# Inverting the triangular matrices of a gated delta rule by 32- and 64-blocks on parts of the PE array

## The chip, the cores and the metric

The kernel runs on one core of one Trainium2 chip. The metric is the device time of one execution in microseconds. Five engines work beside each other, each in the order of its own queue: TensorE (PE; PEld is its loading of weights), VectorE (DVE), ScalarE (ACT), GpSimd (POOL) and SyncE (SP), which here starts the DMAs.

## The reference

The network has two parts of two layers each, for 256 tokens of width 1024 in float32. The changed code serves the mixers of the first part, in which a gated delta rule runs beside a retention. For each of 8 heads and each chunk of tokens the reference solves a unit lower triangular system:

```python
a_mat = jnp.einsum("bhnid,bhnjd->bhnij", kb, kc) * jnp.where(strict, decay_incl, 0.0)
lhs = jnp.eye(CHUNK, dtype=jnp.float32) + a_mat
u = lax.linalg.triangular_solve(lhs, vc * bc, left_side=True, lower=True, unit_diagonal=True)
w = lax.linalg.triangular_solve(lhs, kb * jnp.exp(gc)[..., None], left_side=True, lower=True, unit_diagonal=True)
...
v_new = un - jnp.einsum("bhcd,bhdv->bhcv", wn, S)
o = jnp.einsum("bhcd,bhdv->bhcv", qd, S) + jnp.einsum("bhij,bhjv->bhiv", qkn, v_new)
```

The kernel computes the same with chunks of 128 tokens, so that there are two chunks, and with an explicit inverse of each chunk's 128x128 matrix. Outside the mixers the network has a dense feed-forward layer, a mixture of experts, a gated linear recurrence (hgrn), an attention and two more feed-forward layers; the change does not touch them.

## The kernel before

Weights come from memory in tiles of 1 MB (raw). ScalarE rounds each to whi, VectorE forms the rest wlo (parts, L242 to L265), and every product with a weight is three matmuls of such parts with 256 moving columns, which a program calls ws (L280) and tok (L304). The order of TensorE's instructions is the order of the program, written out by hand; the other engines' queues are ordered by a planner with its own model of costs. Small pieces of work are Python generators in a list; after each half of a projection tick (L135) moves every generator on by one step, so that their matmuls stand between those of the projections.

In a mixer (L457) four pairs p of heads go through three such generators. chains (L486) builds, for each head and chunk, the strictly triangular 128x128 matrix, in U (planes 0 and 2 are the diagonal chunks, plane 1 couples the two chunks). inverses (L494) inverts the 32x32 blocks on the diagonals of two pairs at once on VectorE (invert32, L764) and leaves the blocks in iXc and transposed in iXT. solve (L507) then takes pair by pair. invert_begin (L787) lets GpSimd spread the blocks to block-diagonal 128x128 matrices X and XT and lets VectorE mask U in two ways (Um: what couples 32-blocks, and what couples 64-blocks). invert (L802) then goes up two levels. On each, the product of Um with X and an identity added by a bf16 matmul gives V, which ScalarE evicts; on the first level XT and V give the new X (px), and on both V and XT give the new XT (pxt). Each of these has four matrices of 128x128: two heads and two chunks. gdn_out (L723) uses XT: z is the solution of the first chunk, which changes the right side of the second chunk, and so on. After the first z it begins the next pair (then, L734). The tile z had the same buffer as X.

The steps (yield) of invert separate its groups: one before the first, two between V and px, one each after.

Of the kernel before, what the change touches and what calls it, by code (L numbers as in the profile page):

```python
# [7 lines left out]
F32 = mybir.dt.float32  # L8
# [4 lines left out]
OP = mybir.AluOpType  # L13
# [10 lines left out]

C_ID, C_M, C_TRI, C_NEG, C_IOTA = range(5)
NCONST = 5
C1_LV = 0
C1_GM = 2 * 128
C1_RET = 3 * 128
C1_COS = C1_RET + 4 * 256  # L30
C1_SIN = C1_COS + 256
# [53 lines left out]
class Net:  # L85
# [637 lines left out]
    def gdn_out(self, l, st, begun, then, sgz, p, ga):  # L723
        mp = self.mp
        U, Q, vt, fq = st
        XT = yield from self.invert(*begun)

        z = mp.tile([128, 2, 2, 128], F32, tag="X", name="z", bufs=1)
        pz1 = self.pss("pz1")
        for h in range(2):  # L730
            self.mmul(pz1[:, h * 128:(h + 1) * 128], XT[:, h, 0, :], vt[:, 0, h, :])
        self.act(z[:, 0, :, :], pz1[:, :256].rearrange("p (a b) -> p a b", b=128))
        yield
        then()  # L734
        pz2 = self.pss("pz2")
        for h in range(2):
            self.mmul(pz2[:, h * 128:(h + 1) * 128], U[:, h, 1, :], z[:, 0, h, :])
        v2 = vt[:, 1, :, :]
        self.tt(v2, v2, pz2[:, :256].rearrange("p (a b) -> p a b", b=128), OP.subtract)
        yield  # L740
        pz3 = self.pss("pz3")
        for h in range(2):
            self.mmul(pz3[:, h * 128:(h + 1) * 128], XT[:, h, 1, :], vt[:, 1, h, :])
        self.act(z[:, 1, :, :], pz3[:, :256].rearrange("p (a b) -> p a b", b=128))
        yield

        po = self.pss("pog")
        for h in range(2):
            self.mmul(po[:, h * 128:(h + 1) * 128], Q[:, h, 0, :], z[:, 0, h, :])
            self.mmul(po[:, (2 + h) * 128:(3 + h) * 128], Q[:, h, 1, :], z[:, 0, h, :], start=True, stop=False)  # L750
            self.mmul(po[:, (2 + h) * 128:(3 + h) * 128], Q[:, h, 2, :], z[:, 1, h, :], start=False, stop=True)
        o = mp.tile([128, 1536], F32R, tag="uq", name="go", bufs=4, odd=True)
        o = o[:, :512], o[:, 512:1024]
        while p not in sgz:
            yield

        def tail():
            yield from self.head_out(po, fq, sgz[p].rearrange("p t (h d) -> p t h d", h=2), mp, o, 0,
                                     [self.gdn_g[:, l:l + 1]])
            ga[p] = self.as_act(*o)  # L760

        self.bg.append(tail())

    def invert32(self, n, inv):  # L764


        nc, mp = self.nc, self.mp
        A = self.qk("iA").rearrange("p a b (c i) -> p (a b c) i", i=32)
        X = mp.tile([128, 32, 8], F32, tag="iX", name="iX", bufs=1)
        y = mp.tile([128, 160], F32, tag="iY", name="iY", bufs=1)  # L770
        nc.sync.dma_start(X, self.i["cst4"].rearrange("p (i c) -> p i c", c=8))
        nc.vector.transpose(A.rearrange("p i (b r) -> p i b r", r=4),
                            self.Uc.rearrange("p b i -> p i b")[:, :, :, None].to_broadcast([128, 32, 8, 4]))
        for j in range(31):
            a, m = 31 - j, j // 4 + 1
            yj = y[:, :a * m].rearrange("p (i c) -> p i c", c=m)
            self.tt(yj, A[:, j + 1:, j:j + 1].to_broadcast([128, a, m]), X[:, j:j + 1, :m].to_broadcast([128, a, m]),
                    OP.mult)
            self.tt(X[:, j + 1:, :m], X[:, j + 1:, :m], yj, OP.subtract)
            if j % 5 in (1, 3):  # L780
                yield
        Xc, XTc = (mp.tile([128, 8, 32], F32, tag=t, name=t, bufs=1) for t in ("iXc", "iXT"))
        nc.vector.transpose(Xc.rearrange("p b (c r) -> p c b r", r=4), X.rearrange("p i c -> p c i"))
        nc.vector.transpose(XTc, Xc)
        inv[n] = Xc, XTc

    def invert_begin(self, U, Xc, XTc, p):  # L787

        mp = self.mp
        Ud = U[:, :, 0:3:2, :]  # L790
        gm = self.c1[:, C1_GM:C1_GM + 128].rearrange("p (g i) -> p g i", g=4)[:, None, :, :].to_broadcast([128, 4, 4, 32])
        X, XT = (mp.tile([128, 2, 2, 128], F32, tag=n, name=n, bufs=b) for n, b in (("X", 1), ("XT", 2)))
        Um = [mp.tile([128, 2, 2, 128], F32, tag="Um", name="Um", bufs=2) for _ in range(2)]
        for dst, src in ((X, Xc), (XT, XTc)):
            self.nc.gpsimd.tensor_tensor(dst.rearrange("p a b (g i) -> p (a b) g i", g=4),
                                         src[:, 4 * p:4 * p + 4, None, :].to_broadcast([128, 4, 4, 32]), gm, op=OP.mult)
        for s in range(2):
            lv = self.c1[:, C1_LV + 128 * s:C1_LV + 128 * (s + 1)]
            self.tt(Um[s], Ud, lv[:, None, None, :].to_broadcast([128, 2, 2, 128]), OP.mult)
        return X, XT, Um  # L800

    def invert(self, X, XT, Um):  # L802

        mp = self.mp
        flat = lambda x: x.rearrange("p a b c -> p (a b c)")
        yield
        for s in range(2):
            pv = self.pss("pinv")
            for b in range(4):
                o = pv[:, b * 128:(b + 1) * 128]  # L810
                self.mmul(o, Um[s][:, b // 2, b % 2, :], X[:, b // 2, b % 2, :], start=True, stop=False)
                self.mmul(o, self.idb, self.idb, start=False, stop=True)
            V = mp.tile([128, 2, 2, 128], F32, tag="Um", name="V", bufs=2)
            self.act(flat(V), pv)
            yield
            if not s:
                yield
            if not s:
                px = self.pss("px")
                for b in range(4):  # L820
                    self.mmul(px[:, b * 128:(b + 1) * 128], XT[:, b // 2, b % 2, :], V[:, b // 2, b % 2, :])
                X = mp.tile([128, 2, 2, 128], F32, tag="X", name="X", bufs=1)
                self.act(flat(X), px)
            pt = self.pss("pxt")
            for b in range(4):
                self.mmul(pt[:, b * 128:(b + 1) * 128], V[:, b // 2, b % 2, :], XT[:, b // 2, b % 2, :])
            XT = mp.tile([128, 2, 2, 128], F32, tag="XT", name="XT", bufs=2)
            self.act(flat(XT), pt)
            yield
        return XT  # L830

    def ret_pair(self, l, p, u, w, rq, rk, rv, rg, rets):
# [823 lines left out]
def consts():  # L1656
    import numpy as np
    j = np.arange(128)[:, None]
    i = np.arange(128)[None, :]
    c = np.zeros((128, NCONST, 128), np.float32)  # L1660
# [4 lines left out]
    c[:, C_IOTA] = i  # L1665
    c1 = np.zeros((128, N_C1), np.float32)
    c1[:, C1_GM:C1_GM + 128] = j // 32 == i // 32
    for n in range(2):
        s = 32 << n
        m = (j // (2 * s) == i // (2 * s)) & ((i // s) % 2 == 1) & ((j // s) % 2 == 0)  # L1670
        c1[:, C1_LV + 128 * n:C1_LV + 128 * (n + 1)] = -m.astype(np.float32)
    lg = np.log1p(-np.exp2(-5.0 - np.arange(4)))
    for h in range(4):
        for b in range(2):
# [174 lines left out]
```

## Time and profile before

| | |
|---|---|
| median of 3 runs | 2286.77 us (2286.52 to 2286.87) |
| profiled execution | 2284.09 us |
| its span | 2282.2 us |
| TensorE busy | 2205.0 us, 97% |
| VectorE busy | 1694.3 us, 74% |
| ScalarE busy | 1282.9 us, 56% |
| GpSimd busy | 170.0 us, 7% |

The span runs from the first to the last instruction of the profiled execution. A busy time counts the time in which an engine works on at least one instruction. Matmuls overlap: one with 256 moving columns is listed with 0.28 us, but the next begins 0.12 us later, so the cost of a group of matmuls is read from starts, not from durations. A float32 matmul appears as two records of TensorE. In a form such as `128*32 128x64` the first pair is rows by columns of the array, the second the output. The name of a tile stands without its buffer number.

### The profile page before, as it was taken

What the parts mean: (1) busy time and instruction counts of PE and PEld (TensorE: products, weight loads), DVE (VectorE), ACT (ScalarE), POOL (GpSimd) and SP (SyncE); (2) the same over time, 40 slices, a digit from 0 to 9 for tenths busy, and PEclk for the clock granted to TensorE, in tenths of its full rate; (3) what the DMA queues carried; (4) which work ended last, traced back from release to release, by engine and by line L of the source; (5) the groups of instructions that cost most, each with busy time, mean ns of one, the idle gap of its engine ahead of it and who ended that gap; (6) DMA issues with size and microseconds to landing.
All of it is one profiled execution on the core that took longest, in us unless ns stands there. A gap on an engine that the chain in (4) does not pass through costs nothing.

```text
span 2282.2 us, 38609 instructions
## 1 busy us (share of the span) xinstructions
PE 2205.0 (97%) x15571; PEld 2044.7 (90%) x15571; DVE 1694.3 (74%) x2596; ACT 1282.9 (56%) x1992; POOL 170.0 (7%) x142
## 2 busy tenths in 40 slices
PE   8999999999999999989999999989999999999998
PEld 7998998997899899978888887888898799998997
DVE  6878667776587885679999998686777666666554
ACT  5655545443556554468787776554644555556443
POOL 0032100000003210000000000331000000000000
PEclk9999999999999999999999999999999999999999
DMA  7443566887454356769999996344687564444553
GB/s 235 148 140 122 185 221 209 264 272 257 134 184 147 114 172 200 252 225 370 316 359 335 328 340 235 118 135 149 199 272 277 193 198 147 149 148 139 185 181 133
DMA packets 338525, 478.57 MB, mean 210 GB/s; under 512 B 9874, under 2 KB 239116, under 8 KB 338340
## 3 DMA queue, kind: packets, MB, share of 16 engines
q1 hardware_dynamic: 338340, 476.05, 62.2%
q8 instruction: 123, 2.02, 0.4%
q14 instruction: 62, 0.51, 0.1%
HBM read 474.95 MB, written 1.06 MB: 209 GB/s over the span
## 4 chain that ended last, share of the span: by engine, by line
issue 31%; PE 21%; DVE 2%; POOL 1%; ACT 1%; POOLq 0%; DVEq 0%; ACTq 0%
PE peg L171 5%; PE peu L171 5%; PE pey L171 5%; DVE wlo L159 1%; PE phg L171 1%; PE pgat L171 1%; PE pf L171 1%; PE po L171 1%; PE phv L171 1%; PE phq L171 1%; PE pho L171 1%; POOL ms L346 0%; PE psc L171 0%; POOL rs L177 0%; PE pht L174 0%
## 5 line engine op out<-in xcount | busy, mean ns | idle before, releaser
L159 DVE TENSOR_TENSOR wlo<-raw,whi 128x1024 fp32r<-128x1024 f32 (+2 forms) x802 | 929.7, 1178 | 306.4 <-ACT whi L156 296.8
L156 ACT ACTIVATE whi<-raw 128x1024 fp32r<-128x1024 f32 (+3 forms) x828 | 832.6, 1023 | 517.0 <-PE po L171 61.5
L171 PE MATMUL pu<-uh,whi 128*128 128x256 f32 x480 | 134.6, 280 | 0.0
L171 PE MATMUL pg<-uh,whi 128*128 128x256 f32 x480 | 134.2, 280 | 0.0
L171 PE MATMUL pu<-ul,whi 128*128 128x256 f32 x480 | 134.2, 280 | 0.0
L171 PE MATMUL pg<-ul,whi 128*128 128x256 f32 x480 | 134.1, 279 | 0.0
L171 PE MATMUL pu<-uh,wlo 128*128 128x256 f32 x480 | 133.9, 279 | 0.0
L171 PE MATMUL pg<-uh,wlo 128*128 128x256 f32 x480 | 133.8, 279 | 0.0
L346 POOL TENSOR_SCALAR ms<-ss 128x1 f32<-128x1 f32 x30 | 16.5, 549 | 1485.5 <-ACT junk L156 1479.7
L168 DVE SCALAR_TENSOR_TENSOR acc<-raw,cond,acc 128x1024 f32<-128x1024 f32 x84 | 108.4, 1291 | 17.3 <-DMA raw<-in_ada_w_dram 16.5
L171 PE MATMUL paq<-uh,whi 128*128 128x256 f32 x384 | 111.0, 289 | 0.0
L171 PE MATMUL pqkv<-uh,whi 128*128 128x256 f32 x384 | 108.8, 283 | 0.0
L171 PE MATMUL pqkv<-uh,wlo 128*128 128x256 f32 x384 | 107.1, 279 | 0.0
L171 PE MATMUL paq<-ul,whi 128*128 128x256 f32 x384 | 107.1, 279 | 0.0
L171 PE MATMUL pqkv<-ul,whi 128*128 128x256 f32 x384 | 107.0, 279 | 0.0
L171 PE MATMUL paq<-uh,wlo 128*128 128x256 f32 x384 | 107.0, 279 | 0.0
L171 PE MATMUL po<-whi,fh 128*128 128x512 f32 x264 | 103.1, 391 | 2.0 <-DVE fm L168 2.0
L171 PE MATMUL po<-wlo,fh 128*128 128x512 f32 x264 | 103.0, 390 | 0.7 <-DVE wlo L159 0.7
L171 PE MATMUL po<-whi,fl 128*128 128x512 f32 x264 | 102.8, 389 | 0.0
L171 PEld LDWEIGHTS pg<-uh,whi 128*128 128x128 f32 x480 | 90.2, 188 | 0.9 <-ACT fh L156 0.9
L171 PEld LDWEIGHTS pu<-uh,whi 128*128 128x128 f32 x480 | 90.2, 188 | 0.9 <-ACT whi L156 0.9
L171 PEld LDWEIGHTS pg<-uh,wlo 128*128 128x128 f32 x480 | 90.0, 187 | 0.0
(470 smaller groups left out, 6548.9 us busy)
## 6 DMA issues: line engine op xcount, KB each, us to landing
raw<-in_w_in_dram SPq DMA_DIRECT2D x70, 1024.0 KB
raw<-in_ada_w_dram SPq DMA_DIRECT2D x48, 1024.0 KB
raw<-in_ffn_w_in_dram SPq DMA_DIRECT2D x44, 1024.0 KB
raw<-in_attn_w_in_dram SPq DMA_DIRECT2D x36, 1024.0 KB
raw<-in_exp_w_gate_dram SPq DMA_DIRECT2D x32, 1024.0 KB
raw<-in_exp_w_up_dram SPq DMA_DIRECT2D x32, 1024.0 KB
raw<-in_exp_w_down_dram SPq DMA_DIRECT2D x32, 1024.0 KB
raw<-in_ffn_w_out_dram SPq DMA_DIRECT2D x20, 1024.0 KB
```

Of the source, the lines that this page charges most:

```text
L156: self.nc.scalar.activation(out, in_, func, scale=scale, bias=bias, **k)
L159: self.nc.vector.tensor_tensor(out, a, b, op=op)
L168: self.nc.vector.scalar_tensor_tensor(out, a, s, b, op0=op0, op1=op1)
L171: self.nc.tensor.matmul(out, lhsT, rhs, start=start, stop=stop, skip_group_check=skip)
L346: self.nc.gpsimd.tensor_scalar(ms, self.ss[:, t, 0:1], self.ss[:, t, 1:2], EPS, op0=OP.add, op1=OP.add)
```

## The change

All four matrices' 32-blocks and 64-blocks are now multiplied as such, on the part of the array that the partitions of their operands select. invert_begin makes no Um; GpSimd spreads X only to 64x64 blocks on the first 64 partitions, and XT as before. invert has the same steps with the same four groups: eight 32x32 products of U with iXc directly, negated on the way out of PSUM, one half by ScalarE, the other by VectorE (V); twelve 32x32 products for the new off-diagonal blocks, of X for the upper half alone and of XT for both halves; four 64x64 products for V2; four for the last block of XT. Only new blocks are evicted, into X and XT in place. iXc and iXT have two buffers, z one of its own. The two masks leave the table of constants, whose size stays.

```diff
-        z = mp.tile([128, 2, 2, 128], F32, tag="X", name="z", bufs=1)
+        z = mp.tile([128, 2, 2, 128], F32, tag="z", name="z", bufs=1)
...
-        Xc, XTc = (mp.tile([128, 8, 32], F32, tag=t, name=t, bufs=1) for t in ("iXc", "iXT"))
+        Xc, XTc = (mp.tile([128, 8, 32], F32, tag=t, name=t, bufs=2) for t in ("iXc", "iXT"))
...
     def invert_begin(self, U, Xc, XTc, p):
-        for dst, src in ((X, Xc), (XT, XTc)):
-            self.nc.gpsimd.tensor_tensor(dst.rearrange("p a b (g i) -> p (a b) g i", g=4),
-                                         src[:, 4 * p:4 * p + 4, None, :].to_broadcast([128, 4, 4, 32]), gm, op=OP.mult)
-        for s in range(2):
-            lv = self.c1[:, C1_LV + 128 * s:C1_LV + 128 * (s + 1)]
-            self.tt(Um[s], Ud, lv[:, None, None, :].to_broadcast([128, 2, 2, 128]), OP.mult)
-        return X, XT, Um
+        X = mp.tile([64, 4, 64], F32, tag="X", name="X", bufs=1)
+        XT = mp.tile([128, 2, 2, 128], F32, tag="XT", name="XT", bufs=2)
+        Xc, XTc = (x[:, 4 * p:4 * p + 4, :] for x in (Xc, XTc))
+        for dst, src, n, g in ((X, Xc, 64, 2), (XT.rearrange("p a b c -> p (a b) c"), XTc, 128, 4)):
+            self.nc.gpsimd.tensor_tensor(dst.rearrange("p b (g i) -> p b g i", g=g),
+                                         src[0:n, :, None, :].to_broadcast([n, 4, g, 32]),
+                                         gm[0:n, None, 0:g, :].to_broadcast([n, 4, g, 32]), op=OP.mult)
+        return U, Xc, XTc, X, XT
...
-    def invert(self, X, XT, Um):
+    def invert(self, U, Xc, XTc, X, XT):
         mp = self.mp
-        flat = lambda x: x.rearrange("p a b c -> p (a b c)")
+        T3 = XT.rearrange("p a b c -> p (a b) c")
+        part = lambda b, r, c: U[r, b // 2, 2 * (b % 2), c]
         yield
-        for s in range(2):
-            pv = self.pss("pinv")
+        pv = self.pss("pinv").rearrange("p (b c) -> p b c", b=4)
+        V = mp.tile([128, 4, 32], F32, tag="V", name="V", bufs=1)
+        pairs = [(slice(64 * g, 64 * g + 32), slice(64 * g + 32, 64 * g + 64)) for g in range(2)]
+        for r1, r2 in pairs:
             for b in range(4):
-                o = pv[:, b * 128:(b + 1) * 128]
-                self.mmul(o, Um[s][:, b // 2, b % 2, :], X[:, b // 2, b % 2, :], start=True, stop=False)
-                self.mmul(o, self.idb, self.idb, start=False, stop=True)
-            V = mp.tile([128, 2, 2, 128], F32, tag="Um", name="V", bufs=2)
-            self.act(flat(V), pv)
-            yield
-            if not s:
-                yield
-            if not s:
-                px = self.pss("px")
+                self.mmul(pv[r2, b, 0:32], part(b, r1, r2), Xc[r1, b, :])
+        self.act(V[pairs[0][1]], pv[pairs[0][1], :, 0:32], scale=-1.0)
+        self.ts(V[pairs[1][1]], pv[pairs[1][1], :, 0:32], -1.0)
+        yield
+        yield
+        px = self.pss("px").rearrange("p (b c) -> p b c", b=4)
+        for r1, r2 in pairs:
+            for b in range(4):
+                self.mmul(px[r1, b, 32:64], V[r2, b, :], XTc[r2, b, :])
+            if not r1.start:
                 for b in range(4):
-                    self.mmul(px[:, b * 128:(b + 1) * 128], XT[:, b // 2, b % 2, :], V[:, b // 2, b % 2, :])
-                X = mp.tile([128, 2, 2, 128], F32, tag="X", name="X", bufs=1)
-                self.act(flat(X), px)
-            pt = self.pss("pxt")
-            for b in range(4):
-                self.mmul(pt[:, b * 128:(b + 1) * 128], V[:, b // 2, b % 2, :], XT[:, b // 2, b % 2, :])
-            XT = mp.tile([128, 2, 2, 128], F32, tag="XT", name="XT", bufs=2)
-            self.act(flat(XT), pt)
-            yield
+                    self.mmul(px[r2, b, 0:32], XTc[r2, b, :], V[r2, b, :])
+        self.act(X[pairs[0][1], :, 0:32], px[pairs[0][1], :, 0:32])
+        for r1, r2 in pairs:
+            nc = self.nc
+            (self.act if r1.start else nc.vector.tensor_copy)(T3[r1, :, r2], px[r1, :, 32:64])
+        yield
+        r1, r2 = slice(0, 64), slice(64, 128)
+        pv = self.pss("pinv").rearrange("p (b c) -> p b c", b=4)
+        for b in range(4):
+            self.mmul(pv[r2, b, 0:64], part(b, r1, r2), X[:, b, :])
+        V = mp.tile([128, 4, 64], F32, tag="V2", name="V2", bufs=1)
+        self.act(V[r2], pv[r2, :, 0:64], scale=-1.0)
+        yield
+        pt = self.pss("pxt").rearrange("p (b c) -> p b c", b=4)
+        for b in range(4):
+            self.mmul(pt[r1, b, 0:64], V[r2, b, :], T3[r2, b, r2])
+        self.act(T3[r1, :, r2], pt[r1, :, 0:64])
+        yield
         return XT
```

## Rows read from the trace of the kernel before

**Rows 1.** The page's busy times: us, share of the span, instructions.
```profile
PE 2205.0 (97%) x15571; PEld 2044.7 (90%) x15571; DVE 1694.3 (74%) x2596; ACT 1282.9 (56%) x1992; POOL 170.0 (7%) x142
```

**Rows 2.** Busy time by stretch (PE, PEld, DVE, ACT, POOL), layer 0's inverses.
```profile
160.00:220.00 60.00, 54.79 (x431) 52.35 (x431) 51.38 (x152) 30.12 (x61) 12.70 (x9) 0.97 0.35 108
220.00:310.00 90.00, 88.33 (x761) 87.64 (x760) 60.98 (x92) 44.24 (x75) 13.07 (x9) 1.00 0.61 195
```

**Rows 3.** The tile px: duration in ns (least, median, most), first and last start.
```profile
L156 ACT ACTIVATE X<-px x8: 591/597/599, 190.7 to 892.4; 128x512 f32<-128x512 f32 x8
```

**Rows 4.** TensorE in order of time (start, us, operation), pair 1 of layer 0.
```profile
219.76 0.28 PE L171 MATMUL prv<-whi,ul 128*128 128x256 f32 x1
219.88 0.38 PE L171 MATMUL pinv<-X,Um 128*128 128x128 f32 x2
...
221.32 0.28 PE L171 MATMUL prv<-wlo,uh 128*128 128x256 f32 x1
...
226.74 0.28 PE L171 MATMUL pz<-whi,ul 128*128 128x256 f32 x1
226.86 1.05 PE L171 MATMUL px<-V,XT 128*128 128x128 f32 x8
...
228.64 0.49 PE L174 MATMUL prt<-cst,rsg 128*128 128x128 f32 x3
...
232.80 0.28 PE L171 MATMUL pz<-whi,ul 128*128 128x256 f32 x1
232.91 0.38 PE L171 MATMUL pinv<-X,Um 128*128 128x128 f32 x2
...
234.19 0.65 PE L171 MATMUL pro<-rv,rS 128*128 128x256 f32 x2
...
235.54 1.05 PE L171 MATMUL pxt<-XT,V 128*128 128x128 f32 x8
...
236.55 0.28 PE L171 MATMUL pmg<-ul,whi 128*128 128x256 f32 x1
```

**Rows 5.** TensorE in order of time around hgrn's first product on 32 columns.
```profile
1519.34 0.28 PE L171 MATMUL phv<-whi,ul 128*128 128x256 f32 x1
1519.55 1.09 PE L171 MATMUL pha<-hq,kk 128*32 128x64 f32 x64
1520.57 0.38 PE L171 MATMUL phv<-whi,uh 128*128 128x256 f32 x1
1520.79 0.28 PE L171 MATMUL phv<-wlo,uh 128*128 128x256 f32 x1
```

**Rows 6.** TensorE in order of time, eight records on 64 rows.
```profile
1524.04 1.05 PE L171 MATMUL phs<-hv,hkt 64*128 64x128 f32 x8
```

**Rows 7.** All engines in order of time before pair 0, layers 0 and 1.
```profile
174.72 0.64 DVE L783 STREAM_TRANSPOSE iXc<-iX 128x256 f32<-128x256 f32 x1
...
175.44 2.15 POOL L795 TENSOR_TENSOR X<-iXc,c 128x512 f32<-128x512 f32 x1 [5.31 <-DVE iXc L783]
...
177.65 0.49 PE L171 MATMUL pinv<-X,Um 128*128 128x128 f32 x2 [2.83 <-POOL X L795]
...
773.89 0.49 PE L171 MATMUL pinv<-X,Um 128*128 128x128 f32 x2 [2.82 <-POOL X L795]
```

**Rows 8.** Groups of instructions: busy us, mean ns, idle before and its releaser.
```profile
L159 DVE TENSOR_TENSOR Um<-uq,c 128x512 f32<-128x512 f32 x16 | 12.2, 764 | 0.0
...
L219 DVE COPY col_gdn_gn<-pscol 128x122 f32<-128x122 f32 x1 | 0.3, 278 | 0.0
...
L156 ACT ACTIVATE z<-pz 128x256 f32<-128x256 f32 x16 | 6.0, 376 | 19.6 <-PE pz L171 19.6
```

**Rows 9.** All engines in order of time before px of pair 1.
```profile
220.61 0.76 DVE L878 BATCH_NORM_STATS2 rst<-pro 128x6 f32<-128x256 f32 x2
...
224.26 0.91 ACT L156 ACTIVATE rsg<-rsg,rrr 128x256 f32<-128x256 f32 x2 [6.29 <-POOL rrr L177]
...
225.07 0.58 ACT L156 ACTIVATE V<-pinv 128x512 f32<-128x512 f32 x1
```

More of the change, by code (lines that the diff above doesn't have):

```diff
@@ L26 @@
 NCONST = 5
-C1_LV = 0
-C1_GM = 2 * 128
+C1_GM = 0
 C1_RET = 3 * 128
@@ L789, in invert_begin @@
         mp = self.mp
[L790 to L793, printed above, removed]
-        for dst, src in ((X, Xc), (XT, XTc)):
-            self.nc.gpsimd.tensor_tensor(dst.rearrange("p a b (g i) -> p (a b) g i", g=4),
-                                         src[:, 4 * p:4 * p + 4, None, :].to_broadcast([128, 4, 4, 32]), gm, op=OP.mult)
@@ L797, in invert_begin @@
-        for s in range(2):
-            lv = self.c1[:, C1_LV + 128 * s:C1_LV + 128 * (s + 1)]
-            self.tt(Um[s], Ud, lv[:, None, None, :].to_broadcast([128, 2, 2, 128]), OP.mult)
-        return X, XT, Um
-    def invert(self, X, XT, Um):
+        gm = self.c1[:, C1_GM:C1_GM + 128].rearrange("p (g i) -> p g i", g=4)
+        X = mp.tile([64, 4, 64], F32, tag="X", name="X", bufs=1)
+        XT = mp.tile([128, 2, 2, 128], F32, tag="XT", name="XT", bufs=2)
+        Xc, XTc = (x[:, 4 * p:4 * p + 4, :] for x in (Xc, XTc))
@@ L1667, in consts @@
     c1[:, C1_GM:C1_GM + 128] = j // 32 == i // 32
[L1668 to L1671, printed above, removed]
     lg = np.log1p(-np.exp2(-5.0 - np.arange(4)))
```

## Prediction

> **What bounds the kernel now.** I read the page's busy times first, then the busy times by stretch around the two places where the changed code runs, then the order of TensorE's instructions there, then who waits for whom. TensorE is busy for 97% of the span [rows 1], and in the stretches that hold the inverses for 54.79 of 60 us and 88.33 of 90 us [rows 2]. The order of instructions shows why: the blocks of the inverses stand between the projections' matmuls, which follow each other at 0.12 us, and neither side of a block has a gap. So most of the time that TensorE spends in a block is time of the span. VectorE is the runner-up: 51.38 of 60 us in the first of those stretches, 60.98 of 90 in the second. Layer 1 repeats the pattern some 600 us later, so what I work out for one layer counts twice. There are 8 inverses (4 pairs of heads in 2 layers), as the eight evictions X<-px say [rows 3].
>
> **What TensorE loses.** One inverse is four groups of matmuls. I measure each group as the time from the matmul before it to a matmul behind it, less the ordinary steps of 0.12 us in between. For pair 1 of layer 0 [rows 4]: the first pinv group 1.56 - 0.24 = 1.32 us; px with pxt 1.90 - 0.12 = 1.78; the second pinv group 1.39 - 0.12 = 1.27; the last pxt 1.01 - 0.12 = 0.89. Together 5.26 us in each inverse, for 48 records (an fp32 matmul is two). The other inverses have the same groups of the same length, save where a group waits first.
>
> **What TensorE gets.** New are 8, 12, 4 and 4 fp32 matmuls: 20 with 32 rows, 32 columns of the array and 32 moving columns, 8 with 64 of each; 40 and 16 records in four groups. The trace has no matmul on both part of the rows and part of the columns. The nearest is pha, on 32 columns of the array, half of its records with 64 moving columns and half with 32 [rows 5]. The last phv would be done at 1519.46; the second phv behind the group starts at 1520.79, one step of 0.12 too late for 1520.67. So 64 records cost 1.21 us: 0.09 ahead of the first, 0.10 by which the step after the group is too long, about 0.12 of emptying, and 0.90 for the records. Sixteen of them fall to each of four column tiles, which work beside each other; the 64-wide ones set the pace, so one such record takes its tile 0.90 / 16 = 56 ns.
>
> A record with 64 columns on one tile I therefore take at 56 ns and one with 32 at half of that, 28 ns (an estimate: both the load of the weights and the moving data are half as long). The order written in the code does all four blocks on one tile before it turns to the next, so I count the tiles one after the other: 40 x 28 + 16 x 56 ns = 2.02 us, and for entering and leaving the narrow form 4 x 0.32 = 1.28 us (1.21 - 0.90, rounded up). Sum 3.30 us, 1.96 less than before; for 8 inverses 15.7 us.
>
> Bounds: from below 1.09 / 64 = 17 ns for every record, as on pha's four tiles; that gives 2.23 us and 24.2 us saved. From above the phs row, eight records on one half of the rows: (1.05 - 0.27) / 7 = 0.111 us each [rows 6], no faster than on the whole array. With 56 x 0.111 + 1.28 = 7.5 us the change would lose 2.2 us per inverse, 18 us in all. I take the value near pha, since its tiles are narrow in the dimension that sets the load of the weights, while phs still loads 128 columns.
>
> The Trainium skill has a rule against this: "TensorEngine Tiling (Array Packing)", section "Instruction Overhead", says that a matmul costs about 60 cycles however short, and that a dimension that is already small should not be cut. By that a 32-column record would cost as much as the 64-column one; the trace leaves it open, since in pha the wide records hide the narrow ones. It is the second rival below.
>
> **The wait on GpSimd.** In pair 0 of each layer TensorE stands idle for 2.83 and 2.82 us until GpSimd has spread the inverted 32-blocks into X [rows 7]. That operation takes 2.15 us behind the transpose iXc. The new first group reads iXc itself, done at 174.72 + 0.64 = 175.36, so it can begin about 2.2 us earlier than 177.65. GpSimd's X and XT are first needed a group later, some 10 us on. Gain 2 x 2.2 = 4.4 us. If the planner puts iXc later, the gain is zero; it can't be below that, as the old order waited for iXc as well. That X no longer shares a buffer with z moves GpSimd's work forward, where nobody waits for it; half the partitions and half the elements of X make it shorter, worth nothing on the path. The table of constants keeps its size, so its DMA is the same, and second buffers of iXc and iXT only keep them alive longer.
>
> **What the other engines get.** Gone per inverse are two VectorE masks Um at 764 ns [rows 8] and five ScalarE evictions of 512 elements at 597 ns [rows 3]. Added are two VectorE operations on 32 partitions of 128 elements from PSUM, no row of that shape, the nearest a copy of 122 elements at 278 ns; and on ScalarE three of 128 and two of 256 elements, taken at the 376 ns of z [rows 8], which has 256. VectorE wins about 1 us per inverse, ScalarE about 1.1. This is cover, not gain: neither sets the end of most stretches. But half of V now goes through VectorE: a new wait for TensorE there, with the low parts wlo of the next weights queued behind it, and TensorE's px group waits for that half. Between the first group and px the code leaves two steps, 5.5 us [rows 4], more than one wlo takes, so I cost it at zero, and at up to 1 us per inverse if VectorE is behind by then. The smaller evictions only make later groups' operands ready sooner.
>
> **What is late next.** In pair 1 the eviction of V sits on ScalarE behind rsg, which waits 6.29 us for GpSimd's rrr and so for the statistics rst, which VectorE reaches only at 220.61; V is ready at 225.65 [rows 9], and px on TensorE begins at 226.86. There are 1.2 us of slack. TensorE would come there earlier by 2.2 (wait) + 1.96 (pair 0) + about 0.5 (first group of pair 1) = 4.7 us. That chain hangs on VectorE, which has only about 1.5 us less to do by then. So 4.7 - 1.2 - 1.5 = 2.0 us are given back at px in each layer, 4.0 us in all. Pairs 2 and 3 run where VectorE has a third of its time free; I expect nothing back there.
>
> **Sum.** 15.7 + 4.4 - 4.0 = 16.1 us saved. The profiled execution took 2284.09 us, its span 2282.2; the median of the three runs is 2286.77, 2.7 above, and I take the difference off the median: 2270.7, forecast 2271 us.
>
> **Rivals.**
> 1. The forecast: narrow records cost by their width. 2271, its own range 2265 to 2277. Chance 0.52.
> 2. Narrow records cost as much as 64-wide ones: 40 x 28 ns more per inverse, 9 us in all, 2280. For it: no row shows a 32-wide record alone. Against it: pha starts a record every 17 ns, so nothing in the issue forbids it. Chance 0.13.
> 3. The new hand-over through VectorE binds: px waits 1 us in each inverse, 8 us in all, 2279. For it: VectorE 86% busy in the first stretch, and the in-order queue. Against it: 5.5 us of room in pairs 1 to 3. Chance 0.15.
> 4. Tiles overlap although their matmuls stand one tile after the other: 17 ns a record, 8.6 us more saved, 2262. For it pha's four tiles; against it the order of the code. Chance 0.10.
> 5. Slower: on one tile the load of the weights and the matmul keep the whole array's pace of 0.111 us, as in phs; 18 us lost in the groups instead of 15.7 won, with the 4.4 of the wait about 2300. It decides from about 82 ns a record, where 56 records plus 1.28 us eat both savings. Against it pha's 56 ns. Chance 0.05.
> 6. The change does not shorten the end: the time saved comes back as waits at the next hand-over of the same pair (the second group on X, the last on V2), since TensorE has only one step of matmuls between these. 2284. For it: ScalarE's queue is in order; against it: its evictions get shorter. Chance 0.05.
>
> **Numbers.** This kernel tells a difference from none at about 0.2%, 4.6 us, so faster means under 2282.2. Cases 1 and 4 lie under it whole, 2 and 3 for the most part: 0.83. Within 0.2%: case 6 and the upper parts of 2 and 3, 0.10. Slower: case 5 and what is left, 0.07. The range reaches from case 4, 2260, to beyond cases 2 and 3, 2282.
>
> **What would show it.** Right: the four groups of a pair together at about 3.3 us; no wait of the first pinv group for GpSimd; Um gone from VectorE; px of pair 1 with a wait of about 2 us; all stages after the mixers as long as before. Wrong: 32-wide records stepping at 56 ns or more; px waiting for VectorE's V in pairs 2 and 3; or stretches of the mixers as long as before in spite of shorter groups.

## The result and the profile after

The kernel after takes 2257.49 us (median of 4 runs, 2254.4 to 2259.32), the kernel before beside it 2286.82 (2286.52 to 2286.97): ratio 0.9877, 95% interval 0.9863 to 0.9891, so 25 to 31 us less. The forecast was 2271 with a range of 2260 to 2282: the sign was right, the gain was 1.8 times the forecast, and the time lies below the range. The profiled execution after took 2259.32 us, its span 2257.5; against 2282.2 before, 24.7 us went within the spans. The rest of the 29 us between the medians lies in which execution was profiled: after, the longest of the four; before, one that was 2.7 us under the median. The traces have to explain 24.7.

First the busy times of the page after (us, share of the span, instructions), to hold against [rows 1]:

```profile
PE 2190.3 (97%) x15635; PEld 2025.8 (90%) x15635; DVE 1685.0 (75%) x2596; ACT 1274.2 (56%) x1992; POOL 163.1 (7%) x142
```

TensorE has 64 records more (8 in each inverse, with 40 and 16 narrow ones in place of 48) and is busy 14.7 us less. VectorE and ScalarE lost 9 us each, near the forecast. TensorE's busy time fell by less than the span did, so 10.0 us of the 24.7 were its idle time. That is the first sign that something beside the groups became shorter.

TensorE after, in order of time (start, us, operation); pair 1 of layer 0 as in [rows 4], and the last group of pair 2:

```profile
214.05 0.28 PE L170 MATMUL prv<-whi,ul 128*128 128x256 f32 x1
214.25 0.59 PE L170 MATMUL pinv<-iXc,uq 32*32 32x32 f32 x16
214.77 0.39 PE L170 MATMUL prv<-whi,uh 128*128 128x256 f32 x1
214.99 0.28 PE L170 MATMUL prv<-wlo,uh 128*128 128x256 f32 x1
...
220.22 0.28 PE L170 MATMUL pz<-whi,ul 128*128 128x256 f32 x1
220.43 0.34 PE L170 MATMUL px<-iXT,V 32*32 32x32 f32 x5
...
221.10 0.66 PE L173 MATMUL prt<-cst,rsg 128*128 128x128 f32 x4
...
225.39 0.28 PE L170 MATMUL pz<-whi,ul 128*128 128x256 f32 x1
225.60 0.68 PE L170 MATMUL pinv<-X,uq 64*64 64x64 f32 x8
226.21 1.56 PE L170 MATMUL pro<-rv,rS 128*128 128x256 f32 x6
...
260.80 0.28 PE L170 MATMUL py<-roh,wlo 128*128 128x256 f32 x1
261.01 0.68 PE L170 MATMUL pxt<-XT,V 64*64 64x64 f32 x8
...
261.85 0.28 PE L170 MATMUL py<-rol,whi 128*128 128x256 f32 x1
```

A group comes 0.20 us behind the matmul ahead of it instead of 0.12: the price of entering the narrow form. The second step behind it is 0.22 instead of 0.12, but that belongs only in part to leaving it, since before the step at this place, behind 128-column matmuls on the whole array, was 0.20. Read as in the prediction, from the matmul ahead to one behind less ordinary steps, the groups take 0.94 - 0.24 = 0.70, 0.88 - 0.12 = 0.76, 0.82 - 0.12 = 0.70 and 1.05 - 0.24 = 0.81 us, 2.97 in place of 5.26. Where px and the second pinv group are counted only to the next matmul, the longer step behind them is left out; with it, over all four groups of pair 2 in both traces, 5.33 us became 3.13. So an inverse gives 2.2 us (5.33 - 3.13), and eight give 17.6. The forecast had 1.96 and 15.7.

Next what TensorE waits for in layer 0's mixer: before, from 160 to 346 us (line, what it waited for: us in all, times, longest):

```profile
PE pinv L171 <- POOL X L795: 2.8, 1, 2.8
PE pz L171 <- ACT z L156: 1.7, 1, 1.7
PE pz L171 <- DVE vt L159: 1.4, 1, 1.4
PE py L171 <- DVE go L168: 1.4, 1, 1.4
PE pz L171 <- ACT XT L156: 0.7, 1, 0.7
...
```

The same view of the kernel after:

```profile
PE pro L170 <- DVE uq L167: 1.5, 1, 1.5
PE pz L170 <- ACT z L155: 0.9, 1, 0.9
PE pinv L170 <- DVE iXc L782: 0.7, 1, 0.7
...
```

The sum fell from 8.2 to 3.8 us (the lines left out are 0.2 us before, for rS, and 0.3, 0.2 and 0.2 after, for rS, gms and go). In layer 1 it fell from 7.8 to 5.9: pinv's 2.8, vt's 1.6 and XT's 0.6 went, go's 1.3 became 2.5, uq's 1.5 and iXc's 0.7 came. Two things stand in these lists. The wait of pinv for GpSimd is gone as forecast, but the group runs into a wait that was hidden behind it. And the waits for XT and vt, which the prediction did not name at all, are gone.

All engines after, in order of time ahead of pair 0 (answers to [rows 7]):

```profile
174.47 0.64 DVE L782 STREAM_TRANSPOSE iXc<-iX 128x256 f32<-128x256 f32 x1
...
175.19 1.61 POOL L796 TENSOR_TENSOR X<-iXc,c 64x256 f32<-64x256 f32 x1 [5.31 <-DVE iXc L782]
...
175.26 0.56 PE L170 MATMUL pinv<-iXc,uq 32*32 32x32 f32 x16 [0.69 <-DVE iXc L782]
...
176.50 1.35 DVE L167 SCALAR_TENSOR_TENSOR uq<-pg,gbp,dc 128x256 f32<-128x256 f32 x4
...
177.35 1.92 PE L170 MATMUL pro<-rv,rS 128*128 128x256 f32 x6 [1.53 <-DVE uq L167]
```

The group starts 2.4 us earlier and TensorE then stands 1.53 us before pro, the next matmul in its queue, until VectorE has made another uq. By the code pro does not read uq; uq reads pg, whose PSUM buffer, one of four in the pool, pro seems to take. Of the 2.2 us forecast, 2.8 - 0.7 - 1.5 = 0.6 arrive.

All engines after ahead of px in pair 1 (answers to [rows 9]):

```profile
213.04 0.75 DVE L890 BATCH_NORM_STATS2 rst<-pro 128x6 f32<-128x256 f32 x2
...
213.93 0.18 DVE L158 TENSOR_TENSOR iX<-iX,iY 128x49 f32<-128x49 f32 x1
...
216.65 0.27 ACT L155 ACTIVATE V<-pinv 32x128 f32<-32x128 f32 x1
...
217.70 0.30 DVE L162 TENSOR_SCALAR V<-pinv 32x128 f32<-32x128 f32 x1
```

VectorE reaches rst 7.6 us earlier, the first pinv group starts only 5.6 earlier. V is complete at 218.00 and px starts at 220.43: 2.4 us of slack where a wait of 2.0 was forecast.

From iXc of pair 0 to rst VectorE took 45.9 us before and 38.6 after, 7.3 less. About 2.0 of that is idle time, 1.3 an acc, 0.7 the masks less the new copies, and 3.3 the last 13 steps (iY and iX) of the next 32-block inverse: before, the last of them stands ahead of rst (VectorE before, in order of time):

```profile
217.41 0.17 DVE L159 TENSOR_TENSOR iX<-iX,iY 128x8 f32<-128x8 f32 x1
```

After, all of them stand behind it, from 213.93 on. The forecast had 1.5 us less work there, and the old order.

ScalarE before, in order of time behind the last group of pair 0; pz waited 0.7 us for this XT:

```profile
198.97 0.47 ACT L156 ACTIVATE roh<-prt,ret_g 128x256 fp32r<-128x256 f32 x1 [3.04 <-DVE rol L168]
...
200.77 1.06 ACT L156 ACTIVATE whi<-raw 128x1024 fp32r<-128x1024 f32 x1
201.71 0.59 ACT L156 ACTIVATE XT<-pxt 128x512 f32<-128x512 f32 x1
```

ScalarE after, at the same place:

```profile
193.61 0.47 ACT L155 ACTIVATE roh<-prt,ret_g 128x256 fp32r<-128x256 f32 x1 [0.99 <-DVE rol L167]
...
195.58 0.38 ACT L155 ACTIVATE XT<-pxt 64x256 f32<-64x256 f32 x1
195.86 1.05 ACT L155 ACTIVATE whi<-raw 128x1024 fp32r<-128x1024 f32 x1
```

Left out in both is one whi and th. The planner has put XT ahead of the second whi, and the wait for rol ahead of all this is 2 us shorter. One place outside the mixers changed too: in the feed-forward layer of layer 0 (500 to 530 us) TensorE before had the following wait, and at the same place after it has none of that kind.

```profile
PE po L171 <- DVE fm L168: 2.0, 1, 2.0
```

The account in us of the spans:

| | forecast | traces |
|---|---|---|
| four groups of eight inverses | 15.7 | 17.6 |
| wait of pair 0, twice | 4.4 | 1.2 |
| other waits in the mixers | -4.0 | 5.1 |
| wait in the feed-forward layer | 0 | 2.0 |
| sum | 16.1 | 25.9 |

The spans differ by 24.7, 1.2 less than the sum. The waits in the table are 8.3 of the 10.0 us of idle time; the other 1.7 are small changes elsewhere. Against that, TensorE's busy time fell by 2.9 us less than the groups did. That has the sign of the granted clock, a mean of 0.987 after and 0.989 before: by these means about 59 and 50 us of the spans lie at the lower of its two levels (1.2 and 2.4 GHz), and 9 us more at half the pace cost up to 4.5. Stretches at the lower level lie in other places. Busy times of one window after (PE, PEld, DVE, ACT, POOL), then the granted clock:

```profile
287.00:292.00 5.00, 5.00 (x31) 5.00 (x31) 3.10 (x6) 0.64 (x2) 0.00 (x0) 0.66 0.71 222
```

Before, the clock in this window was 1.00, with 45 matmuls in place of 31. TensorE worked without a gap in both, so the lower level took 14 matmuls of 0.12 us, about 1.7 us. A difference of a few us between two profiles may be that of such stretches.

### The profile page after: what moved, and what is told of

It reads as the page before. It is cut to its first block, busy times and chain, and to the rows that moved or that the text cites. A ratio compares the mean times of both kernels' runs of the same rounds, so it can differ in the third digit from the quotient of the medians.

```text
span 2257.5 us, 38711 instructions
## 1 busy us (share of the span) xinstructions
PE 2190.3 (97%) x15635; PEld 2025.8 (90%) x15635; DVE 1685.0 (75%) x2596; ACT 1274.2 (56%) x1992; POOL 163.1 (7%) x142
## 4 chain that ended last, share of the span: by engine, by line
issue 32%; PE 20%; DVE 3%; POOL 1%; ACT 1%; POOLq 0%; DVEq 0%; ACTq 0%
PE peg L170 5%; PE peu L170 5%; PE pey L170 5%; DVE wlo L158 1%; PE pgat L170 1%; PE po L170 1%; PE phq L170 1%; PE pho L170 1%; PE phg L170 1%; POOL ms L345 0%; PE psc L170 0%; POOL rs L176 0%; PE pht L173 0%; ACT whi L155 0%; PE phv L170 0%
## 5 line engine op out<-in xcount | busy, mean ns | idle before, releaser
L170 PEld LDWEIGHTS pu<-uh,wlo 128*128 128x128 f32 x480 | 90.1, 188 | 0.0
```

The costliest lines, as they stand in the source:

```text
L170: self.nc.tensor.matmul(out, lhsT, rhs, start=start, stop=stop, skip_group_check=skip)
```

## The experiments

Theory A: the gain is the shorter groups on TensorE and whatever the planner's new order does to waits; the relief of VectorE and ScalarE is cover. Rival B: the part that the forecast missed comes from that relief. The kernel after was run again beside the first experiments: 2257.18 us (2254.66 to 2260.15, 5 runs), ratio 0.9884 (0.9865 to 0.9903). It was not run again beside the later ones (from the second level alone on), so there a difference from it is one between sets of runs.

> The changed kernel again, for comparison with the three beside it. All theories: 2254 to 2260 us. If stretches at the lower clock level are what spreads its runs, a run with a higher mean clock is shorter, some 1.7 us per stretch.

The five runs fall in that order but for one: 2260.15 us at a mean clock of 0.987, 2257.18 at 0.988, 2256.65 at 0.989, 2254.66 and 2258.04 at 0.990.

**The masks put back, unused.**

```diff
-C1_RET = 3 * 128
+C1_RET = 128
...
+        for s in range(2):
+            dm = mp.tile([128, 2, 2, 128], BF16, tag="Um", name="Um", bufs=1)
+            lv = self.c1[:, 128 * s:128 * (s + 1)]
+            self.tt(dm, U[:, :, 0:3:2, :], lv[:, None, None, :].to_broadcast([128, 2, 2, 128]), OP.mult)
         return U, Xc, XTc, X, XT
```

> The changed kernel, with the two VectorE masks Um per inverse computed again (nobody reads them; the table of constants is 1 KB per partition smaller to make room). As forecast (VectorE's relief is cover): the same as the changed kernel within 2 us. Rival (VectorE's relief is what took away TensorE's waits for vt, XT, z and go, and what kept px of pair 1 from waiting): 8 x 1.5 us of VectorE work bring back 2 to 4 us in each layer, 4 to 8 us slower than the changed kernel.

2261.62 us (2256.94 to 2265.0, 6 runs), ratio 0.9903 (0.9885 to 0.9922): some 4 us more than the kernel after, with overlapping intervals. That is more than the 2 us of the forecast and at the lower end of the rival's 4 to 8, but not by the rival's way: no wait for vt or XT comes back, and px of pair 1 does not wait. With the masks in its queue VectorE makes iXc at 178.60 us instead of 174.47, and two uq ahead of it. Ahead of pair 0 pinv waits 4.3 us for it, in both layers, in place of 0.7 for iXc and 1.5 for uq: 2.1 us in each layer, about the whole difference. Behind it, in layer 0, from 186 to 284 us, TensorE keeps its distance to the kernel after (3.2 to 3.3 us, of which 0.5 stood before).

**ScalarE's load put back.** Two unused copies of 512 elements in each inverse (627 ns each), behind V and behind V2.

```diff
+        jk = self.tp.tile([128, 512], BF16, tag="junk", name="jk", bufs=2)
+        self.act(jk, self.c1[:, 384:896])
```

> The changed kernel, with two more ScalarE operations of 512 elements per inverse whose result nobody reads, behind the evictions of V and V2, so that ScalarE has about as much to do as before. As forecast (ScalarE's relief is cover): the same as the changed kernel within 2 us. Rival (ScalarE's relief matters, its queue holds z and XT): 2 to 4 us slower than the changed kernel.

2261.23 us (2259.1 to 2261.38, 5 runs), ratio 0.9901 (0.9882 to 0.992), with a span of 2259.6 in the profiled execution, 1.2 above that of the repeated kernel after. The medians differ by 4 us and the intervals overlap. The runs themselves hardly do (2259.1 to 2261.38 against 2254.66 to 2260.15), so a cost of the rival's 2 to 4 us is not ruled out; but in the mixers no wait of TensorE is over 0.5 us longer.

**Both put back.** The two edits together.

> Both additions in one kernel: TensorE's groups and GpSimd's part as in the changed kernel, VectorE and ScalarE loaded as before. As forecast: px of pair 1 waits 2 us in each layer, and the time is 2262 to 2264 us if only that wait returns, or the same as the changed kernel if it doesn't. Rival (relief explains all beyond the groups and the wait for GpSimd, 22 us): 2264 to 2268 us.

2262.38 us (2258.04 to 2264.63, 6 runs), ratio 0.9908 (0.989 to 0.9926). The price does not add up to more than that of the masks. What TensorE waits for in layer 0's mixer of this kernel (160 to 350 us):

```profile
PE pinv L170 <- DVE iXc L782: 4.2, 1, 4.2
PE pz L170 <- ACT z L155: 1.5, 1, 1.5
...
PE py L170 <- DVE go L167: 0.2, 1, 0.2
```

The line left out is 0.3 us for gms. px of pair 1 does not wait, and the median stays under the rival's 2264 to 2268. XT and vt are absent although VectorE and ScalarE carry about their old load (busy 1695.1 and 1283.0 us, 1694.3 and 1282.9 before). So their going is not relief. z is another case: TensorE waits 1.5 us for it here and 1.3 with the masks alone put back, 0.9 in the kernel after.

**The second level alone.** The kernel before, with only the last two groups narrow (64x64 blocks) and the second mask gone.

```diff
...
-        for s in range(2):
+        for s in range(1):
             pv = self.pss("pinv")
...
+        for b in range(4):
+            self.mmul(pv[r2, b, 0:64], U[r1, b // 2, 2 * (b % 2), r2], X3[r1, b, 0:64])
+        V = mp.tile([128, 4, 64], F32, tag="V2", name="V2", bufs=1)
+        self.act(V[r2], pv[r2, :, 0:64], scale=-1.0)
...
+        for b in range(4):
+            self.mmul(pt[r1, b, 0:64], V[r2, b, :], T3[r2, b, r2])
+        self.act(T3[r1, :, r2], pt[r1, :, 0:64])
```

> The kernel before, with the second level alone (the two 64-block groups and their evictions) done as in the changed kernel; the first level keeps its 128x128 products, one mask and the wait for GpSimd. By the length of groups alone: the last two groups of a pair from 1.27 + 0.89 to about 0.69 + 0.80 us, 0.67 us per inverse, 5.4 us below the kernel before. Theory that the planner's new order comes with the shorter last group: TensorE's waits for XT and vt in pair 0 (2.1 us per layer) go as well, 9 to 10 us below. Theory that it needs the first level too: these waits stay, 5 us.

2277.52 us (2273.93 to 2282.88, 10 runs) beside 2283.67 before (2276.13 to 2294.52, 19 runs), ratio 0.9971 (0.9951 to 0.9991): 6 us of the 27, with an interval of 2 to 11 that does not part the theories' 5 and 9 to 10. The lengths of the two groups alone give 0.6 us per inverse, 5 in all. Its waits in layer 0's mixer:

```profile
PE pinv L171 <- POOL X L795: 2.8, 1, 2.8
PE pz L171 <- DVE vt L159: 1.1, 1, 1.1
...
```

The three lines left out are for rsg (0.7), rS and go (0.3 each). XT is gone in both layers, vt still there (1.1 us, 0.9 in layer 1): the wait for XT goes with the second level, most of that for vt needs the first. z is gone as well, and most of go, which the lengths do not count; on the other side the wait for fm in the feed-forward layer is 3.5 us here instead of 2.0.

**The relief alone.** The kernel before without the masks; TensorE multiplies the unmasked U, so the coupling of 32- and 64-blocks is not separated, with the same number of matmuls.

```diff
-        Um = [mp.tile([128, 2, 2, 128], F32, tag="Um", name="Um", bufs=2) for _ in range(2)]
+        Um = [Ud, Ud]
...
-        for s in range(2):
-            lv = self.c1[:, C1_LV + 128 * s:C1_LV + 128 * (s + 1)]
-            self.tt(Um[s], Ud, lv[:, None, None, :].to_broadcast([128, 2, 2, 128]), OP.mult)
```

> The kernel before, without the two masks on VectorE: the products take U unmasked, so what it computes is not the inverse. Only VectorE is relieved, by 16 operations of 764 ns. As forecast (cover): the same as the kernel before within 2 us, with TensorE's waits for XT, vt, z and go as they were. Rival (relief of VectorE takes these waits away): 4 to 8 us below the kernel before.

2283.49 us (2279.62 to 2297.72, 10 runs), ratio 1.0009 (0.999 to 1.0028). Taking 12 us of work off VectorE brings no gain that can be told. In layer 0's mixer pinv waits its 2.8 us, go 1.4, and the two that go in the kernel after are there:

```profile
PE pz L171 <- DVE vt L159: 1.7, 1, 1.7
...
PE pz L171 <- ACT XT L156: 0.4, 1, 0.4
```

The wait of 1.7 us for z is gone, against the expectation. With the unused masks this rules out rival B for XT and vt from both sides. For z it doesn't: its wait is gone without the masks and longer with them, so the 0.8 us that it gave may be relief.

**The early first group taken back.** The first group reads GpSimd's spread X again, which GpSimd now spreads on all 128 partitions.

```diff
-        X = mp.tile([64, 4, 64], F32, tag="X", name="X", bufs=1)
+        X = mp.tile([128, 4, 64], F32, tag="X", name="X", bufs=1)
...
-                self.mmul(pv[r2, b, 0:32], part(b, r1, r2), Xc[r1, b, :])
+                self.mmul(pv[r2, b, 0:32], part(b, r1, r2), X[r1, b, 0:32])
...
```

> The changed kernel, but the first group reads X as GpSimd has spread it (on all 128 partitions) instead of iXc, so TensorE waits for GpSimd in pair 0 again. As forecast: 2.2 us per layer, 4.4 us slower than the changed kernel. Rival, from the trace of the changed kernel (the matmuls pro behind the group now wait 1.5 us for uq on VectorE, so most of what the earlier group won is lost again): 1 to 3 us slower in all.

2256.75 us (2254.48 to 2263.39, 4 runs), ratio 0.9897 (0.9866 to 0.9929): no loss that can be seen. All engines of this kernel ahead of pair 0:

```profile
177.68 1.35 DVE L167 SCALAR_TENSOR_TENSOR uq<-pg,gbp,dc 128x256 f32<-128x256 f32 x4
...
178.04 0.59 PE L170 MATMUL pinv<-X,uq 32*32 32x32 f32 x16 [2.29 <-POOL X L797]
```

pinv waits 2.29 us for GpSimd and pro no longer waits for uq: 2.3 in one place against 0.7 + 1.5 in two. The earlier first group, a term of 4.4 us in the forecast, is worth next to nothing: here the shorter X (1.61 us against 2.15) gives about the same 0.6 us per layer.

**The order of the tiles.** Products of the two halves alternate instead of standing one half after the other.

```diff
-        for r1, r2 in pairs:
-            for b in range(4):
+        for b in range(4):
+            for r1, r2 in pairs:
                 self.mmul(pv[r2, b, 0:32], part(b, r1, r2), Xc[r1, b, :])
```

(and the same for px)

> The changed kernel, with the 32x32 products of the two halves taking turns instead of one half after the other. If tiles work beside each other as far as the order lets them: the first group (16 records, 0.40 us from first to last start) shrinks to about 0.25 us, px (24 records) from 0.45 to 0.3, 0.3 us per inverse, 2.4 us in all, too little for the time to tell. If a tile's records must follow each other whatever stands between: the same lengths as in the changed kernel.

2254.51 us (2253.35 to 2256.03, 4 runs), ratio 0.9877 (0.985 to 0.9905). TensorE of this kernel, pair 1 of layer 0:

```profile
214.17 0.28 PE L170 MATMUL prv<-whi,ul 128*128 128x256 f32 x1
214.37 0.44 PE L170 MATMUL pinv<-iXc,uq 32*32 32x32 f32 x16
214.74 0.39 PE L170 MATMUL prv<-whi,uh 128*128 128x256 f32 x1
...
220.20 0.28 PE L170 MATMUL pz<-whi,ul 128*128 128x256 f32 x1
...
220.78 0.66 PE L173 MATMUL prt<-cst,rsg 128*128 128x128 f32 x4
```

From the matmul ahead to the one behind, the first group takes 0.57 us (0.72 in the kernel after) and px 0.58 (0.88): 0.45 us per inverse, 3.6 in all. The medians differ by 2.7 in the same direction, but the intervals don't part them. It is the lowest median measured.

**The narrow products doubled.** The price of a 32-wide record by itself.

```diff
+                for _ in range(2):
-                self.mmul(pv[r2, b, 0:32], part(b, r1, r2), Xc[r1, b, :])
+                    self.mmul(pv[r2, b, 0:32], part(b, r1, r2), Xc[r1, b, :])
```

(and the same for both products of px)

> The kernel after, with each 32x32 product done twice (40 narrow records more per inverse, the same results). Theory A (narrow records are cheap, and two tiles overlap: 16 records took 0.40 us and 24 took 0.45): the first group grows by about 0.4 to 0.5 us and the px group by 0.45 to 0.7, 0.9 to 1.2 us per inverse, 7 to 10 us in all, near 2266; every other group as before. Theory B (a narrow record costs as much as a 64-wide one, 56 ns): 2.2 us per inverse, 18 us in all, near 2275. Theory C (most of the gain came from the changed order of the other engines' queues, and the length of the groups matters little): less than 4 us.

2266.69 us (2263.57 to 2273.28, 6 runs) beside 2285.96 before (2278.92 to 2293.51, 10 runs), ratio 0.9911 (0.9887 to 0.9935), 9.5 above the kernel after. TensorE of this kernel, pair 1 of layer 0:

```profile
215.63 0.28 PE L170 MATMUL prv<-whi,ul 128*128 128x256 f32 x1
215.84 1.09 PE L170 MATMUL pinv<-iXc,uq 32*32 32x32 f32 x32
...
217.09 0.28 PE L170 MATMUL prv<-wlo,uh 128*128 128x256 f32 x1
...
222.31 0.28 PE L170 MATMUL pz<-whi,ul 128*128 128x256 f32 x1
...
223.95 0.66 PE L173 MATMUL prt<-cst,rsg 128*128 128x128 f32 x4
```

Sixteen records more cost 1.46 - 0.94 = 0.52 us, 24 more 1.64 - 0.88 = 0.76: 32 ns each, with one tile after the other. Both groups grew at or above the upper end of what theory A had, since A counted on the overlap of the halves for every record, and it holds only where one half gives way to the other. Six first groups (in pair 0 the growth lies inside the wait for uq, which is 1.0 us instead of 1.5) and eight px groups make 9.2 us, and the time rose by 9.5 against the kernel after, by 7.5 and 9.7 against the next two kernels, which were run beside this one and have the groups of the kernel after: a microsecond in these groups is about a microsecond of the kernel. That speaks against theory C of the expectation, and 32 ns against its theory B's 56.

**V through ScalarE alone.**

```diff
-        self.ts(V[pairs[1][1]], pv[pairs[1][1], :, 0:32], -1.0)
+        self.act(V[pairs[1][1]], pv[pairs[1][1], :, 0:32], scale=-1.0)
...
-            (self.act if r1.start else nc.vector.tensor_copy)(T3[r1, :, r2], px[r1, :, 32:64])
+            self.act(T3[r1, :, r2], px[r1, :, 32:64])
```

> The kernel after, with both halves of V and both halves of the new XT block evicted by ScalarE. Theory A (the hand-over through VectorE costs nothing, as forecast): within 4 us of the kernel after, px without a wait for V in pairs 1 to 3. Rival (VectorE's queue delays px or the later groups): 1 us per inverse gained, 8 us faster than the kernel after. If ScalarE's two further evictions of 0.27 to 0.32 us come on the path instead, 0.6 us per inverse, 5 us slower.

2259.18 us (2252.93 to 2264.79, 6 runs), ratio 0.9875 (0.9851 to 0.9899): no difference from the kernel after that can be told. The px groups take 0.88 us in both, in all eight inverses, so none waits for V. The new hand-over through VectorE costs nothing that can be told. But a wait of pz for vt is back, 1.3 us in layer 1 and 0.2 in layer 0.

**X in z's buffer again.**

```diff
-        z = mp.tile([128, 2, 2, 128], F32, tag="z", name="z", bufs=1)
+        z = mp.tile([128, 2, 2, 128], F32, tag="X", name="z", bufs=1)
...
-        X = mp.tile([64, 4, 64], F32, tag="X", name="X", bufs=1)
+        X = mp.tile([128, 2, 2, 128], F32, tag="X", name="X", bufs=1)[0:64].rearrange("p a b c -> p (a b c)")[:, 0:256]
+        X = X.rearrange("p (b c) -> p b c", b=4)
```

> The kernel after, with X in z's buffer again, as in the kernel before. Theory A (the buffers are worth nothing, and the waits for XT and vt went because the groups are shorter): within 4 us of the kernel after, no wait of pz for XT, pro waits about 1.5 us for uq. Theory B (the waits for XT, vt and z went because z has a buffer of its own, which frees GpSimd and with it the order of the queues): they come back, 2 us in layer 1 and 3 to 4 in layer 0, 5 to 6 us slower than the kernel after.

2256.99 us (2255.28 to 2261.18, 5 runs), ratio 0.9871 (0.9847 to 0.9895): theory A. No pz waits for XT or vt in either mixer, so they did not go because of the buffers; pro's wait for uq is the 1.5 us expected. In layer 0 another wait has come: the second pinv group of pair 1 stands 0.7 us until ScalarE has evicted XT (0.6 in the kernel with alternating tiles). The kernel after has none there.

## Why the prediction was wrong

**Right: what bounds the kernel, and the groups.** TensorE sets the time, and doubling the narrow products came back about one for one. A record is paid by its width: 58 ns from start to start with 64 columns (forecast 56), 32 with 32 (forecast 28, an estimate). Rows, columns and moving columns halve together here, so which of them sets the price is not shown. Rival 2 (56 ns) and rival 5 (111) are out. Rival 4 too, as a mechanism: where one tile's matmuls stand after the other's the pace is 32 ns, not 17, and its 2262 came nearest the time for another reason. In the 32-wide groups entering and leaving cost less than the 0.32 us taken: the first group is 0.70 us with 16 x 32 ns = 0.51 of records, px 0.86 (pair 0, counted with the step behind) with 0.77, so 0.1 to 0.2, in which the overlap of the halves is included, while the 64-wide groups have 0.81 - 8 x 0.058 = 0.35. The term is 1.9 us too small of 15.7. Rival 6, waits at the pair's own next hand-over, is out for the kernel after, which has none above 0.11 us.

Rival 2 drew on the Trainium skill, "TensorEngine Tiling (Array Packing)", section "Instruction Overhead", by which shortening a matmul below about 60 cycles gains nothing. At 2.4 GHz 60 cycles are 25 ns (an estimate from that page's figure). On one tile the step fell from 58 to 32 ns when the width was halved, so the equal cost that the prediction drew from the rule did not come out, and neither step is short enough to try the rule itself. With two tiles alternating it does not hold from record to record: 16 records are listed with 0.44 us together, the last alone with 0.19, so they start about 17 ns apart.

**Wrong in size: the wait on GpSimd.** 4.4 us were forecast, 1.2 came. The step looked at what releases pinv and not at what the next instruction of TensorE's queue, pro, waits for: uq, which VectorE makes behind iXc and iXT, at a time that no earlier pinv changes. The trace of before shows VectorE at this uq from 176.75 to 178.09 us, just when X was ready, and should have been read for it (VectorE before, in order of time):

```profile
176.75 1.34 DVE L168 SCALAR_TENSOR_TENSOR uq<-pg,gbp,dc 128x256 f32<-128x256 f32 x4
```

The run with GpSimd's X shows that the term was empty.

**The step that failed: what is late next.** It gave back 4.0 us at px of pair 1. It held VectorE's queue fixed but for 1.5 us of work and let TensorE run into it. But in the kernel after the other queues have another order: one acc and 13 steps of the 32-block inverse stand behind rst instead of ahead of it, VectorE reaches rst 7.6 us earlier, V is ready 2.4 us before px, and XT's eviction comes ahead of a whi. No wait grew at px, and 5.1 us of other waits went: vt 3.0, XT 1.3, z 0.8. Together with the 2.0 in the feed-forward layer, 7.1 us are gain that the prediction had at nothing, beside 4.0 that it gave back: 11.1 us of error, of which the oversized wait of pair 0 hides 3.2.

**Right: the cover.** The masks alone were worth nothing that can be told (ratio 1.0009), nor were the hand-over of V through VectorE (rival 3) and the buffers. Put back, the masks cost about 4 us, by making iXc late in pair 0, and ScalarE's load at most about as much.

**Open.** Why the planner moves XT, rst and the uq that it does is not settled: the experiments show that for XT and vt it is neither the load of VectorE and ScalarE nor the buffers, and that XT goes with the second level. Nor is the order the same in all variants: vt is back with V through ScalarE alone, and a wait for XT at another place with X in z's buffer. No kernel was run with the new matmuls and the old order of the other queues, which would show what the order is worth by itself. The wait in the feed-forward layer is gone in all variants with both levels narrow but one, 0.5 us with the products doubled, and longer (3.5) with the second level alone; whether a DMA's arrival decides it was not tried.

## What to carry to other kernels

On a TensorE-bound kernel with small matrices, cut the matmuls to the blocks that are not zero: here the price per record followed the width down to 32, and alternating the tiles made the groups shorter still. When a wait is removed, look at what the next instruction of the same queue needs, its buffer included, before counting it. Where a planner orders the other queues, do not forecast a give-back, or its absence, from the old order: hold it as a range around zero, of the size of all the waits of that stretch (here 8 us in a layer).

## What the runs showed of the hardware that was not expected

Matmuls on different 32x32 tiles run beside each other, but in the program's order only as far as neighbours in the queue are on different tiles: px took 0.88 us with the halves apart and 0.58 alternating, for the same 24 records. Going from whole-array to narrow matmuls costs about 0.09 us ahead of the first; the step of 0.22 us behind the group is hardly longer than the 0.20 behind the 128-column groups of the kernel before. And the time of one kernel follows its mean granted clock: of nineteen runs of the kernel before, the two with 0.986 took 2291.21 and 2294.52 us, the three with 0.991 took 2276.13 to 2279.87.
